# The feed-forward's two products in block form with seven block products for eight, in a two-layer decoder step on one core

## The chip, the cores and the metric

The kernel runs on one core of one Trainium2 chip. The metric is the device time of one execution in microseconds, as the median of several runs. Beside it one execution was taken with a profiler, and all stage times come from that one. Engines are named as in the profile: PE (TensorE matmuls), PEld (its weight loads), DVE (VectorE), ACT (ScalarE), POOL (GpSimd), SP (SyncE, which issues most transfers).

## The reference

One inference step of a decoder of two layers, on 1024 prompt tokens and 8 sample tokens (1032 columns together), with model width 1024 and feed-forward width 4096. Each layer has a token mixer (gated linear attention in layer 0, sliding-window attention in layer 1, each beside attention into a memory), an output projection, and a feed-forward part:

```python
def squared_relu_mlp(h, w_up, w_down):
    return jnp.square(jax.nn.relu(h @ w_up)) @ w_down
...
        x = x + rmsnorm(mix, norm_mix_post[l])
        f = squared_relu_mlp(rmsnorm(x, norm_ffn_pre[l]), w_ffn_up[l], w_ffn_down[l])
        x = x + rmsnorm(f, norm_ffn_post[l])
```

All inputs are float32. Between the layers one projection gives the keys and values for layer 1.

## The kernel before, in words

**Layout.** Activations lie with features on partitions: x is 8 tiles of 128 features, each with 1032 token columns. The columns are cut into three chunks of 384, 384 and 264 (`CH`). A weight tile is 128 x 8 x 128: for one tile of 128 output features (up) it holds all 8 tiles of input features, and for one tile of 128 inner features (down) all 8 tiles of outputs.

**Precision.** Every operand of a large product is split in two parts of type fp32r: a high part, which ACT casts (`wh`, `xh`), and a low part, which DVE makes as the source minus the high part (`wl`, `xl`; function `split`, lines 146 and 147). A product is three matmuls: high by high, high weight by low x, low weight by high x (`proj`, lines 227 to 229). So one up-tile on one chunk is 8 x 3 matmuls.

**The feed-forward (`mlp`).** The 32 tiles of the inner width are taken in eleven groups of two or three (`FF_GROUPS`). For a group, `up` makes the inner rows of one chunk: 24 matmuls per tile into a PSUM buffer, then DVE forms max(p, 0) times r (r is the reciprocal root-mean-square of the token, multiplied in here, line 520), ACT squares it twice, once in float32 and once as the high part, and POOL subtracts for the low part (lines 523 to 525). `down` takes a group's inner rows as moving operand, 3 matmuls per tile and output tile (lines 544 to 546), and DVE adds the result of each output tile to the sum F in SBUF (line 553; ACT copies for the first group, line 550). The order alternates up and down over chunks and groups, so that PE always has a product whose operands have been ready for long. The inner activations never leave SBUF. In layer 0, POOL also multiplies twelve weight tiles of layer 1 by the norm's gains during this stage (`fold`, line 220).

**The closing of a chunk (`Residual`).** ACT squares F, DVE adds up, PE sums over partitions with a matrix of ones (line 185), ACT and DVE make the reciprocal root (lines 188 to 192), DVE scales F, multiplies by the gain and adds the residual, which SP loads from DRAM (lines 294 to 301). In layer 1 the result goes to the output; in layer 0 it is split again as next operand, and `measure` makes the next r.

**What orders the work.** Instructions are written out once, and a planner orders them on each engine by the order in the program, where `high_priority` moves a block ahead by so many instructions (evictions of PSUM by 400, weight loads by `WPRI`, 1500), and it sets the waits. A buffer of a pool is handed on when every user of the tile in it is done. Engines run their own queues in order.

**Buffers.** PSUM has two buffers for products in `pm` and four more in the feed-forward. Weight staging (`wp`) has two raw tiles, `wA` three split ones.

Of the kernel before, what the change touches and what calls it, by code (L numbers as in the profile page):

```python
# [8 lines left out]
F32 = mybir.dt.float32  # L9
# [9 lines left out]
KT = 8  # L19
# [14 lines left out]
FF_GROUPS = [3, 2] + [3] * 9  # L34
# [7 lines left out]
def hybrid_decoder_step(ctx: ExitStack, tc: tile.TileContext, A, O):  # L42
# [37 lines left out]
    mvd = dram.tile([2, P, 2, MEM], F32, tag="mvd", name="mvd")  # L80

# [81 lines left out]
    class Stats:  # L163
        def __init__(self, n, tag="sf"):
            self.n = n
            self.tag = tag
            self.acc = None
            self.extra = []

        def add(self, x):  # L170
            t = view(tp.tile([P, 768], F32, tag="tq", name=nm("tq")), [P, 2, self.n])
            nc.scalar.activation(t, x, AF.Square)
            if self.acc is None:
                self.acc = t
            else:
                TT(self.acc, self.acc, t, ALU.add)  # L176
# [17 lines left out]
    def wload(pool, src, pri=WPRI):  # L194
        with tc.high_priority(pri):
# [4 lines left out]
            split(wh, wl, ws)  # L200
# [15 lines left out]
    def fold(i):  # L216
        src, g = (A["w_kv"][i], G_KV) if i < 4 else (A["w_in_b"][i - 4], G_MIXPRE + 1)
        ws = wp.tile([P, KT, P], F32, tag="ws", name=nm("wf"))
# [22 lines left out]
    class Residual:  # L241
# [22 lines left out]
        def finish(self, bf):  # L264
# [15 lines left out]
            def load(j):  # L280
# [4 lines left out]
                xs = xsp[0].tile([P, 2, 384], F32, tag="xs", name=nm("xs"))[:, :, :n]  # L285
                nc.sync.dma_start(xs, self.xsrc[:, 2 * j : 2 * j + 2, c0 : c0 + n])
                got.append(xs)

            for j in range(4 if self.last else 2):
                load(j)  # L290
            for j in range(4):
# [10 lines left out]
                if j < 2:  # L302
                    load(j + 2)
# [142 lines left out]
    def out_proj(l, make_o, src_pool, st, xsrc, psum=True):  # L446
        wO = st.enter_context(tc.tile_pool(name=nm("wO"), bufs=5, reuse_waits="tile"))
        f0 = st.enter_context(tc.tile_pool(name=nm("fo"), bufs=1, reuse_waits="tile"))
# [30 lines left out]
        f1 = st.enter_context(tc.tile_pool(name=nm("fo"), bufs=1, side="right", reuse_waits="tile"))  # L479
        f2 = st.enter_context(tc.tile_pool(name=nm("fo"), bufs=1, side="right", reuse_waits="tile"))  # L480
        xsp[0] = st.enter_context(tc.tile_pool(name=nm("xs"), bufs=2, side="right", reuse_waits="tile"))
# [8 lines left out]
        R[2].measure(5.5 * unit)  # L490
        set_extra(None, 0)
        return res

    def mlp(l, X):
        with ExitStack() as st:
            xsp[0] = st.enter_context(tc.tile_pool(name=nm("xs"), bufs=2, side="right", reuse_waits="tile"))
            fp = st.enter_context(tc.tile_pool(name=nm("ff"), bufs=1, side="right", reuse_waits="tile"))
            ap = st.enter_context(tc.tile_pool(name=nm("fa"), bufs=6, reuse_waits="tile"))
            wB = st.enter_context(tc.tile_pool(name=nm("fw"), bufs=4, reuse_waits="tile"))
            set_extra(st.enter_context(tc.tile_pool(name=nm("pmx"), bufs=4, space=PSUM, reuse_waits="tile")), 4)  # L500
            F = [fp.tile([P, KT, CH[c][1]], F32, tag=f"f{c}", name=nm("f")) for c in (2, 1, 0)][::-1]
            groups = []
            m0 = 0
            for g in FF_GROUPS:
                groups.append(list(range(m0, m0 + g)))
                m0 += g
            ups, dns, acts = {}, {}, {}

            def up(gi, c):
                if c == 0:  # L510
                    ups[gi] = [wload(wA, A["w_up"][l, m]) for m in groups[gi]]
                hl, r = X[c]
                n = CH[c][1]
                res = []
                for w in ups[gi]:
                    ps = mmps()
                    proj(ps, w, hl, n)
                    with first():
                        t = tmp3([P, 2, n])
                        STT(t[:, 0, :], ps[:, :n], 0.0, r, ALU.max, ALU.mult)  # L520
                        ah = ap.tile([P, n], F32R, tag="ah", name=nm("ah"))
                        al = ap.tile([P, n], F32R, tag="al", name=nm("al"))
                        nc.scalar.activation(t[:, 1, :], t[:, 0, :], AF.Square)  # L523
                        nc.scalar.activation(ah, t[:, 0, :], AF.Square)  # L524
                        nc.gpsimd.tensor_tensor(al, t[:, 1, :], f32(ah), ALU.subtract)  # L525
                    res.append((ah, al))
                acts[gi, c] = res

            R = {}

            def down(gi, c):
                if gi == L:
                    R[c] = Residual(c, F[c], G_FFNPOST + l, xd, last=(l == 1))
                if c == 0:
                    dns[gi] = [wload(wB, A["w_down"][l, m]) for m in groups[gi]]
                n = CH[c][1]
                a = acts.pop((gi, c))
                ng = len(a)
                for m in range(KT):
                    ps = mmps()  # L540
                    for k in range(ng):
                        wh, wl = dns[gi][k]
                        ah, al = a[k]
# [4 lines left out]
                    if gi == 0:  # L548
                        with first():
                            nc.scalar.copy(F[c][:, m, :], ps[:, :n])  # L550
# [932 lines left out]
```

## Time and profile before

| | |
|---|---|
| median of 3 runs | 2422.64 us (2418.98 to 2424.86) |
| the profiled execution | 2415.36 us |
| its span, first to last instruction | 2413.6 us |
| granted TensorE clock, mean | 0.99 |
| feed-forward of layer 0 | from 544.4 to 1271.2 us |
| feed-forward of layer 1 | from 1668.7 to 2395.8 us |

A row of the profile's groups has the line of the code, the engine, the operation, its output and inputs with their shapes, the count, then busy time, the mean of one in ns, and the idle time before it with what ended it. In a row by time the first number is the start, the second the duration in us. In a row by stretch come the stretch and its length, then the busy time and the count on PE, PEld, DVE, ACT and POOL, the granted clock, the DMA share and GB/s. A matmul's duration overlaps that of the next one; what it costs is the distance from start to start.

### The profile page before, as it was taken

The numbers are of one execution on the slowest core, as the hardware profiler recorded it, in microseconds if no ns is written. First come the engines' busy times: TensorE is split into PE (matmuls) and PEld (weight loads), VectorE is DVE, ScalarE is ACT, GpSimd is POOL, SyncE is SP. The second block draws the span as 40 slices with busy tenths as digits, with TensorE's granted clock in tenths as the row PEclk, the third lists the DMA queues.
The fourth block names the chain that finished last, engine by engine and source line by source line (L and its number), as shares of the span: only waits on it lengthen the run. The fifth ranks groups of instructions, "written<-read, shape, count | busy, mean of one in ns | idle before, by whom it ended". The sixth has DMA issues, their size and how long they took to land. (4 is left out here: it accounts for less than half of the span.)

```text
span 2413.6 us, 36268 instructions
## 1 busy us (share of the span) xinstructions
PE 2338.5 (97%) x14996; PEld 2221.0 (92%) x14996; DVE 1140.8 (47%) x2180; ACT 816.8 (34%) x1762; POOL 267.5 (11%) x270
## 2 busy tenths in 40 slices
PE   7999999899999999999998999899999999999997
PEld 6769998899999999999998878599999999999997
DVE  7544547666333333333368355647333333333337
ACT  6442535445222112221234355545422121221224
POOL 0001100002122112211110000200111111111121
PEclk9999999999999999999999999999999999999998
DMA  5321016433122122211125101324211111111123
GB/s 195 127 86 56 20 62 157 129 122 116 62 88 71 62 79 88 88 53 36 53 67 158 49 18 46 98 70 141 63 53 36 53 53 53 53 33 38 53 63 114
DMA packets 82799, 184.64 MB, mean 77 GB/s; under 512 B 7754, under 2 KB 49811, under 8 KB 82339
## 3 DMA queue, kind: packets, MB, share of 16 engines
q1 hardware_dynamic: 69522, 156.27, 20.9%
q0 software_dynamic: 3312, 13.30, 1.8%
q10 hardware_dynamic: 9792, 12.68, 1.4%
q8 instruction: 119, 1.95, 0.3%
q14 instruction: 54, 0.44, 0.1%
HBM read 150.79 MB, written 33.51 MB: 76 GB/s over the span
## 5 line engine op out<-in xcount | busy, mean ns | idle before, releaser
L227 PE MATMUL mm<-xh,wh 128*128 128x384 f32 (+3 forms) x1344 | 434.5, 324 | 18.2 <-ACT wh L146 12.0
L227 PE MATMUL mx<-xh,wh 128*128 128x384 f32 (+2 forms) x1344 | 430.4, 320 | 4.2 <-ACT wh L146 2.3
L228 PE MATMUL mx<-xl,wh 128*128 128x384 f32 (+2 forms) x1344 | 430.6, 321 | 3.5 <-DVE xl L598 2.0
L229 PE MATMUL mm<-xh,wl 128*128 128x384 f32 (+3 forms) x1344 | 432.1, 322 | 0.3 <-DVE wl L147 0.3
L228 PE MATMUL mm<-xl,wh 128*128 128x384 f32 (+3 forms) x1344 | 431.8, 321 | 0.0
L229 PE MATMUL mx<-xh,wl 128*128 128x384 f32 (+2 forms) x1344 | 430.2, 320 | 0.0
L146 ACT CAST wh<-ws 128x1024 fp32r<-128x1024 f32 x186 | 193.1, 1049 | 584.8 <-PE mx L228 204.6
L525 POOL TENSOR_TENSOR al<-t,ah 128x384 fp32r<-128x384 f32 (+1 forms) x192 | 204.5, 1065 | 1550.1 <-ACT ah L524 1349.8
L545 PE MATMUL mx<-al,wh 128*128 128x384 f32 (+1 forms) x1015 | 321.4, 317 | 0.3 <-POOL al L525 0.3
L544 PE MATMUL mx<-ah,wh 128*128 128x384 f32 (+1 forms) x1015 | 321.4, 317 | 0.0
L546 PE MATMUL mx<-ah,wl 128*128 128x384 f32 (+1 forms) x1015 | 321.1, 316 | 0.0
L147 DVE TENSOR_TENSOR wl<-ws,wh 128x1024 fp32r<-128x1024 f32 x186 | 226.8, 1229 | 115.1 <-ACT wh L146 115.0
L523 ACT ACTIVATE t<-t 128x384 f32<-128x384 f32 (+1 forms) x192 | 94.0, 490 | 544.5 <-DVE t L520 544.4
L227 PEld LDWEIGHTS mm<-xh,wh 128*128 128x128 f32 (+2 forms) x1344 | 249.6, 186 | 28.9 <-ACT wh L146 12.5
L228 PEld LDWEIGHTS mx<-xl,wh 128*128 128x128 f32 (+1 forms) x1344 | 253.3, 188 | 7.0 <-DVE xl L598 3.6
L227 PEld LDWEIGHTS mx<-xh,wh 128*128 128x128 f32 (+1 forms) x1344 | 253.1, 188 | 6.6 <-ACT wh L146 2.5
L553 DVE TENSOR_TENSOR f<-mx,f 128x384 f32<-128x384 f32 (+1 forms) x318 | 162.6, 514 | 202.5 <-PE mx L546 202.0
L229 PEld LDWEIGHTS mm<-xh,wl 128*128 128x128 f32 (+2 forms) x1344 | 249.4, 186 | 8.7 <-issue 6.5
L228 PEld LDWEIGHTS mm<-xl,wh 128*128 128x128 f32 (+2 forms) x1344 | 250.0, 186 | 7.5 <-issue 5.4
L229 PEld LDWEIGHTS mx<-xh,wl 128*128 128x128 f32 (+1 forms) x1344 | 253.1, 188 | 1.6 <-issue 1.0
L520 DVE SCALAR_TENSOR_TENSOR t<-mx,r 128x384 f32<-128x384 f32 (+1 forms) x131 | 67.5, 516 | 338.5 <-PE mx L229 320.7
L545 PEld LDWEIGHTS mx<-al,wh 128*128 128x128 f32 x1015 | 190.4, 188 | 0.7 <-POOL al L525 0.5
(370 smaller groups left out, 3301.5 us busy)
## 6 DMA issues: line engine op xcount, KB each, us to landing
ws<-in_w_up SPq DMA_DIRECT2D x64, 512.0 KB, 3.7
ws<-in_w_down SPq DMA_DIRECT2D x64, 512.0 KB, 3.7
ws<-in_w_in_a SPq DMA_DIRECT2D x22, 512.0 KB, 3.7
xd<-f ACTq DMA_DIRECT2D x24, 384.0 KB, 4.7
ws<-in_w_out SPq DMA_DIRECT2D x16, 512.0 KB, 3.7
xs<-xd SPq DMA_DIRECT2D x16, 384.0 KB, 4.2
wfd<-wf SPq DMA_DIRECT2D x12, 512.0 KB, 2.6
ws<-wfd SPq DMA_DIRECT2D x12, 512.0 KB, 3.9
```

The costliest lines, as they stand in the source:

```text
L146: nc.scalar.copy(hi, src)
L147: (eng or nc.vector).tensor_tensor(lo, src, f32(hi), ALU.subtract)
L227: nc.tensor.matmul(ps[:M, :n], wh[:, k, :M], xh[:, k, :], start=(k == 0), stop=False)
L228: nc.tensor.matmul(ps[:M, :n], wh[:, k, :M], xl[:, k, :], start=False, stop=False)
L229: mm = nc.tensor.matmul(ps[:M, :n], wl[:, k, :M], xh[:, k, :], start=False, stop=(k == KT - 1))
L520: STT(t[:, 0, :], ps[:, :n], 0.0, r, ALU.max, ALU.mult)
L523: nc.scalar.activation(t[:, 1, :], t[:, 0, :], AF.Square)
L525: nc.gpsimd.tensor_tensor(al, t[:, 1, :], f32(ah), ALU.subtract)
L544: nc.tensor.matmul(ps[:, :n], wh[:, m, :], ah, start=(k == 0), stop=False)
L545: nc.tensor.matmul(ps[:, :n], wh[:, m, :], al, start=False, stop=False)
L546: mm = nc.tensor.matmul(ps[:, :n], wl[:, m, :], ah, start=False, stop=(k == ng - 1))
L553: TT(F[c][:, m, :], ps[:, :n], F[c][:, m, :], ALU.add)
```

## The change

Both products of the feed-forward are computed in 2 x 2 blocks by the form of Winograd, with seven block products and fifteen block sums in the place of eight block products. This holds for 28 of the 32 tiles of the inner width, in 14 pairs (`PAIRS`); the first four tiles (`NPL`) are computed as before, at the beginning of the up-product and at the end of the down-product. The up-product of all pairs comes first, then the down-product; the squared inner rows go to DRAM (`awd`, and `apd` for the four plain tiles) and are read back.

**Up.** The weight of a pair is 2 x 2 blocks (two output tiles by two halves of the input features), x is 2 x 2 blocks (two halves of the features by two halves of the columns, 516 each; the columns are those of chunks 0 and 1, and the two halves of chunk 2). The combinations of x are made once per layer: x is first scaled by gain and r (`scale`, on ACT and POOL, for chunk 2 on DVE), then combined in place and split seven times (`steps`, in a wide piece of 384 columns and a narrow one of 132). The combinations of the weights are made for each pair on POOL (`wino_weights`), each followed by a split on ACT and DVE. A block product is 4 x 3 matmuls on each of two halves of 258 columns (`SUB`).

**Down.** The pairs are taken in groups of 3, 3, 3, 3 and 2 (`DGROUPS`). A phase is one of the seven block products of a group, over four output tiles and two halves: 8 PSUM buffers of 3 x 3 matmuls (or 2 x 3). For each phase and pair the weight block is combined (POOL) and split, the block of inner rows is combined (POOL) and split. Seven sums of 4 x 516 are kept in SBUF; DVE adds each PSUM buffer to them. In the last group the seven sums are combined into the four blocks of the output (`phase`, 28 additions on DVE). Then the four plain tiles run over the three chunks, and DVE adds the blocks on eviction.

```diff
+NPL = 4
+HALF = NT // 2
+SUB = HALF // 2
+PAIRS = [(m, m + 1) for m in range(NPL, DFF // P, 2)]
+DGROUPS = [list(range(j, min(j + 3, len(PAIRS)))) for j in range(0, len(PAIRS), 3)]
+ORDER = (1, 7, 6, 5, 2, 3, 4)
...
+    class Slots:
...
+        def next(self):
+            self.half ^= 1
+            if self.half == 0:
+                self.cur = (self.kept or self.makers)[self.i % len(self.makers)]
+                if not self.kept:
+                    self.cur = self.cur()
+                self.i += 1
+            ks = slice(4 * self.half, 4 * self.half + 4)
+            return self.cur[0][:, ks, :], self.cur[1][:, ks, :]
...
+    def wino_weights(a11, a12, a21, a22, slots):
+        PT = nc.gpsimd.tensor_tensor
+
+        def cut(x):
+            hi, lo = slots.next()
+            split(hi, lo, x)
+            return hi, lo
+
+        yield cut(a11)
+        PT(a11, a11, a21, ALU.subtract)
+        PT(a21, a21, a22, ALU.add)
+        yield cut(a11)
+        PT(a11, a22, a11, ALU.subtract)
+        yield cut(a11)
+        yield cut(a21)
+        w = cut(a12)
+        PT(a12, a12, a11, ALU.subtract)
+        yield w
+        yield cut(a12)
+        yield cut(a22)
...
+        def steps(p):
+            cut(1, "b11", p)
+            comb(p, "b12", "b22", "b12", ALU.subtract)
+            yield
+            cut(7, "b12", p)
+            comb(p, "b11", "b12", "b11", ALU.add)
+            yield
...
+        def triple(ps, wh, wl, hl_of, n):
+            for k in range(n):
+                xh, xl = hl_of(k)
+                nc.tensor.matmul(ps, wh(k), xh, start=(k == 0), stop=False)
+                nc.tensor.matmul(ps, wh(k), xl, start=False, stop=False)
+                mm = nc.tensor.matmul(ps, wl(k), xh, start=False, stop=(k == n - 1))
+            tick(mm, 3 * n * SUB)
...
+        def product(j, i, a, tmp):
...
+            for s in range(2):
+                ps = mmps()[:, :SUB]
+                triple(ps, lambda k: wh[:, k, :], lambda k: wl[:, k, :],
+                       lambda k: (sub(hi[:, k], s), sub(lo[k], s)), 4)
+                with first():
...
+                    elif i == 6:
+                        TT(sub(t("u4", "tq"), s), ps, sub(tmp["p1"], s), ALU.add)
+                        TT(sub(tmp["u3"], s), ps, sub(tmp["u3"], s), ALU.add)
...
+            with first():
+                for cc in {5: [c22], 2: [c11], 3: [c12], 4: [c21]}.get(i, []):
+                    STT(cc, cc, 0.0, cc, ALU.max, ALU.mult)
...
+            prepare(t + (3 if j == 0 else 7))
+            product(j, i, a, tmp)
+            if i == ORDER[-1]:
+                nc.sync.dma_start(awd[l, j], a)
...
+            def prep(self, i):
+                PT = nc.gpsimd.tensor_tensor
...
+                for q, gen in enumerate(self.gens):
+                    b11, b12, b21, b22 = self.blocks[q]
+                    w = next(gen)
+                    if i == 7:
+                        PT(b12, b22, b12, ALU.subtract)
+                    if i == 6:
+                        PT(b11, b12, b11, ALU.add)
+                    if i == 5:
+                        PT(b12, b22, b11, ALU.subtract)
+                    x = {1: b11, 7: b12, 6: b11, 5: b12, 2: b21, 3: b22, 4: b21}[i]
+                    h = homes[q]
+                    split(h[:, 0], h[:, 1], x)
+                    if i == 2:
+                        PT(b21, b11, b21, ALU.subtract)
+                    out.append((w, h))
+                return out
...
+            for mp in range(4):
+                for s in range(2):
+                    ps = mmps()[:, :SUB]
+                    triple(ps, lambda q: parts[q][0][0][:, mp, :], lambda q: parts[q][0][1][:, mp, :],
+                           lambda q: (sub(parts[q][1][:, 0], s), sub(parts[q][1][:, 1], s)), n)
+                    dst = sub(acc[i][:, mp], s)
                     with first():
...
+                        if gi == 0:
+                            nc.scalar.copy(dst, ps)
+                        else:
+                            TT(dst, ps, dst, ALU.add)
+            if gi != last:
+                return
+            for mp in range(4):
+                c = lambda k: acc[k][:, mp]
+                if i == 6:
+                    TT(c(6), c(6), c(1), ALU.add)
+                    TT(c(7), c(7), c(6), ALU.add)
...
+        for t in range(len(phases) - 1):
+            prep_phase(t + 1)
+            phase(t)
```

Smaller edits: the six weight tiles of the next projection (`wload` with `eng`) have their low parts made on POOL and not on DVE; the statistics of chunk 2 before the feed-forward are asked for 3.5 instead of 5.5 tile-products later; the residual is loaded to buffers that the feed-forward has freed; the output projection's result stays in SBUF, since the blocks of x are made from it.

476 lines of the change are left out of this document (376 added, 100 removed).

## The prediction

> **What bounds the kernel now.** I read the page from the top, then the stages around the feed-forward, then the distance from one matmul to the next, and last the groups by shape on the engines that get new work.
>
> ```profile
> span 2413.6 us, 36268 instructions
> PE 2338.5 (97%) x14996; PEld 2221.0 (92%) x14996; DVE 1140.8 (47%) x2180; ACT 816.8 (34%) x1762; POOL 267.5 (11%) x270
> ...
> PEclk9999999999999999999999999999999999999998
> ...
> 544.40:571.00 26.60, 24.78 (x132) 24.14 (x131) 21.04 (x34) 14.67 (x27) 3.77 (x3) 0.94 0.52 154
> 571.00:1200.00 629.00, 627.58 (x4023) 627.20 (x4022) 228.00 (x368) 143.41 (x260) 112.61 (x97) 1.00 0.21 70
> 1200.00:1271.30 71.30, 70.59 (x468) 69.68 (x467) 42.23 (x68) 22.88 (x35) 8.32 (x9) 1.00 0.22 71
> ```
>
> The last three rows are layer 0's feed-forward (stretch, its length, then busy PE, PEld, DVE, ACT, POOL, the granted clock, the DMA share, GB/s). PE is busy for 627.58 of 629.00 us at clock 1.00, and DVE for 228 of them. The stage, 544.40 to 1271.30, is 726.9 us of PE at work, and everything else hides under it. So fewer matmul columns shorten it, until another engine fails to keep up. "Busy" doesn't say what a matmul costs, since matmuls overlap; the distance between starts does:
>
> ```profile
> 799.79 0.33 PE L227 MATMUL mm<-xh,wh 128*128 128x384 f32 x1
> ...
> 801.70 0.34 PE L229 MATMUL mm<-xh,wl 128*128 128x384 f32 x1
> 801.87 0.28 PE L544 MATMUL mm<-ah,wh 128*128 128x264 f32 x1
> ...
> 805.96 0.28 PE L545 MATMUL mx<-al,wh 128*128 128x264 f32 x1
> ...
> 53.34 0.28 PE L227 MATMUL mx<-mh,wh 128*128 128x256 f32 x1
> ...
> 54.41 0.28 PE L227 MATMUL mx<-mh,wh 128*128 128x256 f32 x1
> ```
>
> Twelve matmuls of 384 columns lie from the first row to the second: 1.91 us over 11 steps, 0.1736 us each. From 801.87 to 805.96 are 34 steps of 264 columns, 0.1203 us. The 256-column stream in the last two rows makes 9 steps in 1.07 us, 0.119 us. The new products have 258 columns, between the last two: I take 0.119.
>
> **The change part by part.** PE first. Before, each layer has, for each of the two products, 32 tiles by 8 by 3 matmuls on each of three chunks: 3072 of 384 columns and 1536 of 264 columns in all, 533.3 + 184.8 = 718.1 us; the stage's 726.9 holds 8.8 us more (statistics, gaps), which I keep. After: four plain tiles in both products, 384 x 0.1736 + 192 x 0.1203 = 89.8 us; and 14 pairs by 7 products by 4 blocks by 2 halves by 3, twice, 4704 matmuls x 0.119 = 559.8 us. Together 649.6: PE has 68.5 us less per layer, 137 us in both. That is only 9.5% of the stage, not one eighth of 28/32, because the count of matmuls grows with 258 columns in the place of 384.
>
> A rule stands against this. The Trainium skill, page "TensorE: Matmul & The Clock Gate", section "Back-to-back issue gap", gives for sustained weight-load and matmul pairs about 81 ns at 128 columns and 131 ns at 512. Estimated from these by a straight line, 384, 264 and 258 columns would cost 114, 99 and 98 ns, the layer 502 us before and 524 after: slower. The rows above (174 and 120 ns) disagree.
>
> What goes on the other engines (relu products, squares and the 240 sums of a layer) was hidden under PE, so its going is worth nothing by itself. What they get instead is priced from these groups (busy, then mean ns of one):
>
> ```profile
> L147 DVE TENSOR_TENSOR wl<-ws,wh 128x1024 fp32r<-128x1024 f32 x186 | 226.8, 1229 | 115.1 <-ACT wh L146 115.0
> L147 DVE TENSOR_TENSOR xl<-f,xh 128x768 fp32r<-128x768 f32 x8 | 7.6, 949 | 0.8 <-ACT xh L146 0.8
> L553 DVE TENSOR_TENSOR f<-mx,f 128x264 f32<-128x264 f32 x108 | 46.3, 432 | 57.6 <-PE mx L546 57.5
> L146 ACT CAST wh<-ws 128x1024 fp32r<-128x1024 f32 x186 | 193.1, 1049 | 584.8 <-PE mx L228 204.6 <-PE mm L228 149.8 <-PE mx L545 78.3
> L525 POOL TENSOR_TENSOR al<-t,ah 128x384 fp32r<-128x384 f32 x128 | 134.5, 1051 | 1135.6 <-ACT ah L524 980.0 <-DVE xl L311 133.1 <-issue 22.5
> L946 POOL TENSOR_TENSOR qk<-qk,tq 96x512 f32<-96x512 f32 x8 | 10.3, 1283 | 13.4 <-ACT tq L931 13.4
> L220 POOL TENSOR_TENSOR wf<-wf,gains 128x1024 f32<-128x1024 f32 x12 | 22.8, 1898 | 59.6 <-DMA wf<-in_w_in_b 34.5 <-DVE t L520 23.0 <-DMA wf<-in_w_kv 1.5
> ...
> 2380.34 1.82 DVE L296 TENSOR_TENSOR f<-f,xall 128x768 f32<-128x768 f32 x2
> 2382.07 1.51 DVE L294 TENSOR_TENSOR f<-f,rf 128x768 f32<-128x768 f32 x1
> ...
> 2381.34 1.43 POOL L525 TENSOR_TENSOR al<-t,ah 128x264 fp32r<-128x264 f32 x1 [25.97 <-ACT ah L524]
> ...
> 1257.17 1.77 DVE L147 TENSOR_TENSOR wl<-ws,wh 128x1024 fp32r<-128x1024 f32 x1
> ...
> 1257.04 0.82 POOL L525 TENSOR_TENSOR al<-t,ah 128x264 fp32r<-128x264 f32 x1 [27.46 <-ACT ah L524]
> ```
>
> DVE from SBUF is 0.949 us for 768 and 1.229 for 1024 elements, so 0.67 for the new 512 and 516; in a row each is some 0.04 shorter (two of 768 take 1.82), I use 0.63. An eviction of 258 columns: 0.42 alone, 0.38 in a row. ACT: 0.6 for 512. POOL: 1.28 for 512, the L946 row.
>
> The last five rows hold the point that matters most. A DVE operation with two SBUF inputs that starts while POOL works is late by what POOL has left: the split at 1257.17 took 1.77 instead of 1.23 us (POOL ended at 1257.86), the product at 2382.07 took 1.51 instead of 0.91 (POOL until 2382.77). POOL suffers as well: 1.43 us behind two DVE operations, 0.82 where it came first. So POOL's combinations and DVE's splits take turns. The Trainium skill, "SBUF — State Buffer", section "Who interferes with whom", states this as a lock held for a whole instruction; the trace agrees with it on operations with two SBUF inputs. If it were no lock, the slower rival below would lose its mechanism.
>
> *Up-product.* Per pair: 16 evictions, 4 squares (516), 7 weight splits (512) on DVE, 16 x 0.38 + 11 x 0.63 = 13.0 us; POOL 4 x 1.28 and in layer 0 a fold of 1.9, 7.0 us; PE 168 x 0.119 = 20.0. Turns on the shared path 11 x 0.63 + 7.0 = 13.9. The splits are issued seven products ahead. All is hidden: 0 per layer, at most 10 if a pair waits 0.7 us.
>
> *Its start.* The blocks of x are scaled, combined and split while four plain tiles run (44.9 us) and in the first pair (20). DVE: five splits and four combinations of the wide piece, 10 x 0.95 + 4 x 1.82 = 16.8; the same of the narrow one and its scaling, about 11 by the 264-column row; the pair's own 13.0; and what already keeps DVE busy there, 21.04 of 26.60 us in the first stretch. Together some 62 of 65 us, with POOL in turns (8 scalings between 1.3 and 1.9 us, two splits). Between 0 and 20; I take 6, since PE is reached only by the last part of it. Chunk 2's statistics are asked for two tile-products sooner (3.5 for 5.5): chunk 0's plain tiles cover them, 0, at most 2 inside this bound.
>
> *Between the products.* The down-product's first blocks go to the homes of the last block of x, free two products (5.7 us) before the end; its weights' slot is that of the last product. The nearest transfers:
>
> ```profile
> ws<-in_w_up SPq DMA_DIRECT2D x64, 512.0 KB, 3.7
> ...
> xs<-xd SPq DMA_DIRECT2D x8, 264.0 KB, 3.7
> ```
>
> The loads (264 KB each, then 512 KB) take 3.7 us, more when nine queue up; then ACT 0.6, and nine POOL operations (11.5 us) before the second phase, whose forerunner lasts 8.6. Between 1 and 15, I take 5. The activations' way out and back adds 30 MB per layer, 45 GB/s on top of 70, under the 154 of the first stretch: hidden, or at most inside the 15.
>
> *Down-product, four groups of three pairs.* A phase is 72 matmuls, 8.57 us. DVE: six splits and eight evictions, 6 x 0.63 + 8 x 0.38 = 6.8 us. POOL: 24 combinations per group, 30.7 us, in bursts (9, 6, 3, 6 in four of seven phases). Taking turns: 42 x 0.63 + 30.7 = 57.2 of 60.0 us. The chain POOL, ACT, DVE runs one phase ahead of PE. It fits by 3 us on the mean, not in the bursts: the 9 take 11.5 us plus DVE's turns against about 12 us from the middle of the phase before. Also every second phase waits to split its third weight, whose slot is shared with a half of the phase just ending. Nothing if DVE goes between, up to 10 per group; I take 2.5, near the lower end because the mean fits: 10.
>
> *Last group, of two pairs.* A phase is 48 matmuls, 5.71 us; DVE needs 4 x 0.63 + 8 x 0.38 = 5.6, and the block sums come on top: 8, 8, 4 and 4 operations of 0.63 after phases three to six. The next phase's splits queue behind them on DVE, and PE waits for those: 4.9 + 4.9 + 2.4. Then the plain tiles' splits (4 x 1.23 + 2 x 0.95) and the sums against one phase: 6.7. Sum 18.9, with POOL's turns up to 28; at least 10 if sums are put off. I take 20.
>
> *Plain tiles, tail, hand-over.* Chunk 1's closing work has 11.5 us of matmuls (96 x 0.1203) as cover where it had 17.3; POOL instead of DVE splits the next layer's six weights (six turns of 1.9 us, hidden by 25 us of the first chunk's matmuls). 0 to 8; I take 3.
>
> Losses per layer: 0 + 6 + 5 + 10 + 20 + 3 = 44 against 68.5, bounds 11 and 121. Net 24.5, 49 us in both: the span goes to 2364.6 and its execution (2415.36, 1.8 above its span) to 2366.4. The median of the runs, 2422.64, lies 7.3 above that execution; on its scale the time is 2373.6, **2374 us**, 2.0% less.
>
> **The rivals.** *PE stays the bound.* If DVE and POOL slot in as smoothly as now (228 busy of 629), only the low bounds remain: 2422.6 - 2 x (68.5 - 11) = 2308, at best 2286. For it: PE's 99.8% now. Against it: the last group's sums alone exceed their cover. *DVE blocked by POOL becomes the down-product's bound: slower.* Let x be the share of POOL's 30.7 us per group in which DVE stands still. DVE then needs 42 x 0.63 + 56 x 0.38 = 47.7 and 30.7x against 60, the bound from x = 0.4; four groups lose 4 x (30.7x - 12.3), the last 18.9 + 20.5x. With 14 us for the rest the 68.5 are used up at x = 0.59; at 0.7 the loss is 84 per layer and the time 2454, at 0.8 it is 2483. For it: the two delayed rows. Against it: evictions can run beside POOL. *A matmul costs mostly its issue, not its columns.* Then 5280 matmuls in the place of 4608 outweigh: at the mean distance of now the layer's 718 us become 823, and the time 2633 before any loss. The three streams speak against it; only a weight load that is slower in these products could bring it. (By the figures of the Trainium skill's page "TensorE: Matmul & The Clock Gate" above, the two layers would take 44 us longer than before: some 2467.) *The count isn't reduced*: the loops fix it; time as before.
>
> **How the numbers follow.** Forecast 0.53, own range 2335 to 2425; PE-bound 0.20; blocked DVE 0.24; issue-bound 0.02; not as said 0.01. A measurement of this kernel can tell about 0.3% (7 us) from no change. Faster: 0.49 of the forecast and PE-bound, 0.69. Within 0.3%: the forecast's upper edge 0.04, the third case's lower edge 0.02, and the last 0.01, 0.07. Slower 0.24. The range leaves out half of the PE-bound case and a tenth at the top: 2300 to 2445.
>
> **What would show it.** Right: 258-column matmuls 0.119 us apart; up-stretches with PE gaps only in the first pair; in the down-product gaps ended by DVE's splits (or POOL), 2 to 3 us per full group, some 20 in the last. Wrong: gaps in every phase ended by DVE with splits near 1.2 us instead of 0.67 (blocked DVE), steps over 0.125 us (issue), or none at all in the last group (PE-bound). A transfer that lands late between the products would add what I have not priced.

## The result and the profile after

The kernel after takes 2476.24 us (median of 4 runs, 2474.82 to 2477.93), the kernel before on the same chip 2420.81 (2416.91 to 2424.86): ratio 1.0229, 95% interval 1.0209 to 1.0249. It is slower, where the forecast was 2374 us and faster. The profiled execution took 2475.34 us.

First the page after: the span, the engines, the granted clock in 40 slices.

```profile
span 2473.6 us, 41200 instructions
PE 2276.5 (92%) x16340; PEld 2138.5 (86%) x16340; DVE 1760.0 (71%) x3214; ACT 967.3 (39%) x2098; POOL 651.9 (26%) x460
...
PEclk9999999999999998999998999999899998999988
```

PE has fallen from 97% to 92% of a longer span: it works less, as intended, and stands more. POOL went from 267.5 to 651.9 us. Where PE stands is read from layer 0's stages (stretch, length, then busy PE, PEld, DVE, ACT, POOL, clock, DMA share, GB/s):

```profile
546.00:611.00 65.00, 50.71 (x297) 49.64 (x296) 59.37 (x78) 33.13 (x60) 26.98 (x13) 0.89 0.37 118
611.00:649.00 38.00, 26.87 (x174) 24.93 (x173) 36.20 (x52) 13.90 (x32) 20.66 (x15) 0.87 0.40 132
...
720.00:922.00 202.00, 201.98 (x1684) 201.74 (x1683) 135.36 (x273) 46.27 (x90) 55.42 (x41) 1.00 0.34 119
922.00:955.50 33.50, 22.79 (x148) 21.16 (x148) 16.38 (x18) 12.76 (x29) 21.72 (x15) 0.80 0.73 277
...
999.00:1197.00 198.00, 187.15 (x1513) 184.68 (x1512) 184.97 (x292) 68.22 (x126) 110.60 (x72) 0.98 0.28 86
1197.00:1250.50 53.50, 46.66 (x339) 45.18 (x338) 50.66 (x103) 16.67 (x28) 16.82 (x10) 0.90 0.06 21
1250.50:1303.30 52.80, 49.46 (x293) 47.99 (x292) 43.26 (x74) 17.28 (x22) 2.42 (x1) 0.94 0.44 136
```

These are the plain up-tiles, the first pair, ten pairs in the steady state, the passage between the products, groups 2 to 4 of the down-product, the last group, and the plain down-tiles. Of these stages only the steady up-product (201.98 of 202.00) keeps PE full. In groups 2 to 4 DVE is busy for 184.97 of 198 us and POOL for 110.60, where before DVE had 228 of 629.

Against what the matmuls alone need, by the starts of the block matmuls in the trace (0.120 us a step, 20.1 us a pair of the up-product, 60.3 a full group, 40.2 the last one, 44.9 the plain tiles of a product):

| us beyond the matmuls | forecast (bounds) | layer 0 | layer 1 |
|---|---|---|---|
| plain up-tiles, then up-product | 6 (0 to 30) | 20.1 + 28.7 | 17.2 + 12.5 |
| between the products (first two phases) | 5 (1 to 15) | 16.0 | 15.3 |
| the rest of the four full groups | 10 (0 to 40) | 17.8 | 17.8 |
| last group | 20 (10 to 28) | 13.1 | 14.4 |
| plain down-tiles, then hand-over or tail | 3 (0 to 8) | 7.8 + 12.7 | 9.6 + 2.0 |
| sum | 44 | 116.2 | 88.8 |

The last two columns also hold the 8.8 us per layer that the old stage had beyond its matmuls; so 116.2 + 88.8 - 2 x 8.8 = 187.4 us are lost. PE saves 718.1 - 654.2 = 63.9 us per layer at 0.120 us a step, 127.8 in both. The difference, 59.6, fits the 60.0 us by which the span grew (2473.6 - 2413.6), as well as rounded steps allow, which is to 2 or 3 us.

What PE waited for most in groups 2 to 4 of layer 0 (total, times, longest):

```profile
PE mx L709 <- DVE wl L154: 6.1, 4, 2.5
```

Of PE's 10.8 us of waits there, 10.3 end with one of DVE's splits. By the starts of the matmuls, the steps that hold a wait lose 12.9 us, and slower steps behind them 4.2 (see the last section).

DVE's instructions in the same stretch, by shape (count, then busy, mean ns):

```profile
L154 DVE TENSOR_TENSOR af<-ar,af 128x516 fp32r<-128x516 f32 x63 | 68.3, 1084 | 0.0
L901 DVE TENSOR_TENSOR acc<-mx,acc 128x258 f32<-128x258 f32 x111 | 44.5, 416 | 6.7 <-PE mx L709 6.6
L154 DVE TENSOR_TENSOR wl<-arw,wh 128x512 fp32r<-128x512 f32 x41 | 44.4, 1082 | 2.7 <-ACT wh L153 2.7
L154 DVE TENSOR_TENSOR wl<-ws,wh 128x512 fp32r<-128x512 f32 x21 | 25.0, 1192 | 0.2 <-ACT wh L153 0.2
```

The 125 splits take 137.7 us, 1.10 each, where the forecast had 0.67 alone and 0.63 in a row. Why, a stretch of group 2 shows, row by row (start, duration), DVE first, then POOL:

```profile
1030.59 1.74 DVE L154 TENSOR_TENSOR af<-ar,af 128x516 fp32r<-128x516 f32 x1
1032.26 0.41 DVE L901 TENSOR_TENSOR acc<-mx,acc 128x258 f32<-128x258 f32 x1
1032.59 1.67 DVE L154 TENSOR_TENSOR wl<-arw,wh 128x512 fp32r<-128x512 f32 x1
```

```profile
1030.48 1.30 POOL L569 TENSOR_TENSOR ws<-ws,ws 128x512 f32<-128x512 f32 x1 [13.48 <-DVE wl L154]
1032.41 1.30 POOL L859 TENSOR_TENSOR ar<-ar 128x516 f32<-128x516 f32 x1 [0.63 <-DVE af L154]
1034.40 1.29 POOL L569 TENSOR_TENSOR arw<-arw 128x512 f32<-128x512 f32 x1 [0.69 <-DVE wl L154]
```

Each of these splits starts 0.1 to 0.2 us after a POOL combination and ends about 0.55 us after that combination does: POOL's 1.30, then the split's own work. The eviction behind it, which reads one operand from PSUM and is not slowed itself (0.41), waits in DVE's queue until the split is done. A split on DVE releases the next combination, which is in place, and the next split runs into that again.

### The profile page after: what moved, and what is told of

Same layout as the page of the kernel before. It is cut to its first block, busy times and chain, and to the rows that moved or that the text cites. A ratio compares the mean times of both kernels' runs of the same rounds, so it can differ in the third digit from the quotient of the medians.

```text
span 2473.6 us, 41200 instructions
## 1 busy us (share of the span) xinstructions
PE 2276.5 (92%) x16340; PEld 2138.5 (86%) x16340; DVE 1760.0 (71%) x3214; ACT 967.3 (39%) x2098; POOL 651.9 (26%) x460
## 5 line engine op out<-in xcount | busy, mean ns | idle before, releaser
L153 ACT CAST wh<-ws 128x512 fp32r<-128x512 f32 (+1 forms) x286 | 202.3, 721 | 586.4 <-POOL ws L569 109.7
L154 DVE TENSOR_TENSOR wl<-ws,wh 128x512 fp32r<-128x512 f32 (+1 forms) x280 | 267.3, 956 | 176.2 <-ACT wh L153 173.9
L708 PE MATMUL mx<-af,wh 128*128 128x258 f32 x1034 | 300.6, 291 | 14.2 <-DVE af L154 14.2
L235 PE MATMUL mm<-xh,wh 128*128 128x384 f32 (+3 forms) x904 | 296.3, 328 | 15.8 <-ACT wh L153 12.7
L709 PE MATMUL mx<-af,wl 128*128 128x258 f32 x1034 | 299.5, 290 | 9.9 <-DVE wl L154 9.9
L707 PE MATMUL mx<-af,wh 128*128 128x258 f32 x1034 | 296.5, 289 | 9.0 <-ACT af L153 7.1
L708 PE MATMUL mx<-xf,wh 128*128 128x258 f32 x792 | 227.8, 288 | 9.4 <-DVE xf L154 9.4
L707 PE MATMUL mx<-xf,wh 128*128 128x258 f32 x792 | 228.1, 288 | 5.7 <-DVE u L746 4.3
L709 PE MATMUL mx<-xf,wl 128*128 128x258 f32 x792 | 227.2, 287 | 5.4 <-DVE wl L154 5.4
L708 PEld LDWEIGHTS mx<-af,wh 128*128 128x128 f32 x1034 | 203.2, 197 | 17.0 <-DVE af L154 17.0
L709 PEld LDWEIGHTS mx<-af,wl 128*128 128x128 f32 x1034 | 203.3, 197 | 11.9 <-DVE wl L154 11.9
L707 PEld LDWEIGHTS mx<-af,wh 128*128 128x128 f32 x1034 | 200.0, 195 | 10.4 <-ACT af L153 7.3
L154 DVE TENSOR_TENSOR af<-ar,af 128x516 fp32r<-128x516 f32 x194 | 203.6, 1055 | 1.2 <-ACT af L153 0.8
L235 PEld LDWEIGHTS mm<-xh,wh 128*128 128x128 f32 (+1 forms) x904 | 167.7, 186 | 26.0 <-ACT wh L153 12.7
L708 PEld LDWEIGHTS mx<-xf,wh 128*128 128x128 f32 x792 | 153.4, 194 | 10.5 <-DVE xf L154 10.5
L707 PEld LDWEIGHTS mx<-xf,wh 128*128 128x128 f32 x792 | 152.9, 193 | 6.6 <-DVE u L746 4.7
```

What stands on the lines that cost most here:

```text
L153: nc.scalar.copy(hi, src)
L154: (eng or nc.vector).tensor_tensor(lo, src, f32(hi), ALU.subtract)
L235: nc.tensor.matmul(ps[:M, :n], wh[:, k, :M], xh[:, k, :], start=(k == 0), stop=False)
L707: nc.tensor.matmul(ps, wh(k), xh, start=(k == 0), stop=False)
L708: nc.tensor.matmul(ps, wh(k), xl, start=False, stop=False)
L709: mm = nc.tensor.matmul(ps, wl(k), xh, start=False, stop=(k == n - 1))
```

## The experiments

The theory, **turns** (A in the expectations): DVE's splits and POOL's combinations take turns on a shared path, and DVE's queue stands meanwhile. The rivals: **POOL's results** (C), for which the splits wait, and not for its turn; **transfers and buffers**, which hold PE up; and **DVE's own work** (B), too much for it. Each run is one execution unless said otherwise. The kernel before took 2420.29 us beside e1 to e4, and 2411.95 beside e5 to e8, so whole times from the two sets compare only to within some 8 us; the stages are surer.

**e1_no_comb.** All combinations on POOL are left out (weights and inner rows); splits, transfers and matmuls stay.

```diff
-        PT = nc.gpsimd.tensor_tensor
+        PT = lambda *x: None
...
-                PT = nc.gpsimd.tensor_tensor
+                PT = lambda *x: None
```

> All combinations of weight blocks and inner-row blocks on POOL are left out in the block products (the blocks are split and multiplied uncombined). Theory A, POOL's operations hold up DVE's splits: the down-product's splits fall from about 1.1 us to 0.67 to 0.70, groups two to four of the down-product take 181 us together (198 in the changed kernel), the first two phases lose under 4 us in the place of 16, the last group still loses 10 or more by its sums; the whole about 2400 us. Theory B, DVE has too much work of its own: the splits fall too, but groups two to four stay over 190 us. Theory C, PE waits for POOL's results and not for DVE's lock: 181 us as in A, but e2 must then show the same.

Measured: 2394.5 us. Groups 2 to 4 of layer 0, DVE by shape and then the stretch:

```profile
L901 DVE TENSOR_TENSOR acc<-mx,acc 128x258 f32<-128x258 f32 x115 | 48.6, 424 | 23.3 <-PE mx L709 22.9
L154 DVE TENSOR_TENSOR af<-ar,af 128x516 fp32r<-128x516 f32 x61 | 42.0, 688 | 0.0
L154 DVE TENSOR_TENSOR wl<-arw,wh 128x512 fp32r<-128x512 f32 x42 | 28.7, 684 | 4.7 <-ACT wh L153 4.7
...
L154 DVE TENSOR_TENSOR wl<-ws,wh 128x512 fp32r<-128x512 f32 x22 | 15.0, 683 | 0.5 <-ACT wh L153 0.5
```

```profile
980.00:1160.00 180.00, 180.00 (x1506) 180.00 (x1505) 139.98 (x296) 68.53 (x128) 0.00 (x0) 1.00 0.29 95
```

The same 125 splits take 85.7 us, 0.69 each: 52.0 us less, 17.3 per group. PE is busy for 180.00 of 180.00; groups 2 to 4 last 60.3 us each. So neither transfers and buffers nor DVE's own work (139.98 of 180) bound the full groups of the kernel after. The evictions didn't change (0.424 against 0.416). The two phases between the products lose 8.2 and 4.9 us instead of 16.0 and 15.3, so about half of that loss or more is POOL's. The up-product, whose weight blocks go uncombined as well, takes about 294 and 289 us instead of 311 and 295, though the folds are still on POOL. The plain up-tiles did not change (66.2 and 62.1; after 65.0 and 62.1), nor did the last group much (52.0 and 50.7; after 53.3 and 54.6): these losses have other causes than the combinations.

**e2_comb_idle.** The down-product's combinations run on POOL as in the kernel after, but write to a spare tile that nothing reads; the blocks go uncombined into the product.

```diff
-        PT = nc.gpsimd.tensor_tensor
+        PT = lambda o, a, b, op: nc.gpsimd.tensor_tensor(o2(o) if o2 else o, a, b, op)
```

> In the down-product POOL makes every combination from the same sources but writes it to a spare tile that nobody reads; the blocks are multiplied uncombined. Theory A: POOL still takes turns with DVE, splits stay over 1.0 us and groups two to four take 190 us or more. Theory C: nobody waits for POOL's results any more, so groups two to four fall to about 181 us although the splits stay long. Up-product as in the changed kernel.

Measured: 2481.1 us.

```profile
L154 DVE TENSOR_TENSOR af<-ar,af 128x516 fp32r<-128x516 f32 x62 | 66.4, 1072 | 0.0
```

```profile
1000.00:1200.00 200.00, 186.64 (x1495) 184.16 (x1495) 180.09 (x292) 64.86 (x121) 107.37 (x70) 0.97 0.27 85
```

Nobody waits for POOL's results, and still the splits take 1.07 us and groups 2 to 4 last 66.6 to 69.9 us (after 64.6 to 67.8). So it is POOL's activity beside DVE, not the wait for its data: the turns hold, and the wait for POOL's results falls as cause in the full groups. (Why they are even a little longer than in the kernel after isn't shown. Buffers are still handed on only when POOL has read them, as in the kernel after.) Between the products it is otherwise: the first two phases lose 12.5 and 12.1 us here, 16.0 and 15.3 in the kernel after, 8.2 and 4.9 in e1. Of POOL's share, 3.5 and 3.2 us are thus the wait for its results, and 4.3 and 7.2 its activity.

**e3_comb_dve.** The combinations are made on DVE.

```diff
-        PT = nc.gpsimd.tensor_tensor
+        PT = nc.vector.tensor_tensor
...
-                PT = nc.gpsimd.tensor_tensor
+                PT = nc.vector.tensor_tensor
```

> The same combinations made on DVE in the place of POOL. Theory A: nobody shares the path, each costs DVE 0.63 us, a full group needs 62.8 us of DVE against 60 of PE, so groups two to four take 188 to 192 us (198 now), the first two phases lose 8 in the place of 16, the last group loses 5 to 10 more; the whole 2440 to 2465 us. Theory B: DVE is fuller still, groups two to four 205 us or more, the whole over 2480.

Measured: 2418.75 us, better than any theory had it.

```profile
L154 DVE TENSOR_TENSOR af<-ar,af 128x516 fp32r<-128x516 f32 x60 | 41.1, 687 | 0.1
...
L859 DVE TENSOR_TENSOR ar<-ar,ar 128x516 f32<-128x516 f32 x6 | 4.1, 687 | 0.0
```

```profile
985.00:1165.00 180.00, 180.00 (x1497) 179.38 (x1496) 174.93 (x356) 67.86 (x123) 0.00 (x0) 1.00 0.30 95
```

DVE has 336 instructions more over the run and is busy for 174.93 of 180 us, and PE is full again: the groups last 60.4 to 60.9. A combination on POOL costs DVE 0.72 us of standing (17.3 us for 24), and 0.69 to do it itself (the second row). Handing this work to POOL relieved DVE of nothing.

**e4_fold_act.** Only the multiplication of layer 1's weights by the gains (12 tiles, during layer 0) goes from POOL to ACT.

```diff
-        nc.gpsimd.tensor_tensor(ws, ws, gains[:, g, :].unsqueeze(2).to_broadcast([P, KT, P]), ALU.mult)
+        for k in range(KT):
+            nc.scalar.mul(ws[:, k, :], ws[:, k, :], gains[:, g, k : k + 1])
```

> The twelve weight tiles of the next projections are multiplied by their gains on ACT (eight operations of 128 columns each) in the place of POOL. Theory A: layer 0's up-product loses the 16 us or more that it takes longer than layer 1's (310.9 against 294.7 us for the block products), the whole 2455 to 2462 us. Theories B and C: DVE's own work or the block chain sets the start, the up-product stays over 305 us and the whole within 5 us of 2476.

Measured: 2462.7 us, 12.6 less than the profiled execution of after. Layer 0's up-product shrank from 310.9 to 298.0 us; the other stages stayed within 2.5 us. What the folds meet is seen in the kernel after, in POOL's groups from 546 to 649:

```profile
L228 POOL TENSOR_TENSOR wf<-wf,gains 128x1024 f32<-128x1024 f32 x5 | 15.4, 3079 | 7.7 <-DVE xl L331 6.5 <-DMA wf<-in_w_kv 1.2
L619 POOL TENSOR_TENSOR f<-f,r 128x768 f32<-128x768 f32 x6 | 12.4, 2088 | 26.8 <-ACT t L609 26.8
```

Five folds, 3.08 us each where they took 1.9 before, stand in the same turns as the blocks of x. Without the combinations and with the folds (e1) the up-product was shortened by as much, so POOL's load as a whole counts there, not the folds alone.

**e5_no_sums.** The 28 sums of a layer that combine the seven block sums are left out.

```diff
-            if gi != last:
-                return
+            return
```

> The changed kernel without the 28 additions that combine the seven sums in the last group (the output blocks stay uncombined). If the sums before the next phase's splits on DVE cause the last group's loss, as the prediction has it, the group takes 41 to 43 us instead of 53 to 55, the plain tiles behind it lose 2 to 4 us less, and the whole is 25 to 32 us faster (2445 to 2451). If POOL's turns cause it, the group stays at 48 us or more.

Measured: 2445.8 us. The last group lasts 42.9 us in both layers (after 53.3 and 54.6), the plain down-tiles 46.1 and 48.4 (52.7 and 54.5). So the sums cost 17.0 and 17.8 us per layer, three fifths of it in the last group and the rest after it. The whole is 29.6 us shorter and not 34.8, as layer 0's up-product and the hand-over came out 2.8 and 2.6 us longer.

**e6_start.** e3 with the fold on ACT as in e4, and the scaling of chunks 0 and 1 and all low parts of x on DVE. POOL is all but idle in the feed-forward (2.87 us from 545 to 1250).

```diff
-            if c < 2:
+            if False:
...
-            eng = nc.gpsimd if i in (2, 3) else nc.vector
+            eng = nc.vector
```

> As e3 (combinations on DVE), and POOL is taken out of the start: the fold on ACT, the scaling of x and all splits of its blocks on DVE. If POOL's turns make the start late, the plain tiles fall from 65.7 to about 55 us and the first pair from 38 to under 30 us, in layer 0 more than in layer 1; the whole 2385 to 2398 us against 2419 of e3. If DVE's own work bounds the start (it gets some 25 us more of it per layer), the gain is under 8 us, or the start is longer.

Measured: 2387.4 us. The plain up-tiles fell from 65.7 and 61.9 (e3) to 48.6 and 47.7. The up-product fell from about 302 to 297 us in layer 0 and rose from 294 to 297 in layer 1. In layer 1 of e3 the scaling and the low parts of x were all that POOL had in these tiles (there is no fold there), so taking them off POOL brought the 14.2 us; ACT's part of the scaling went to DVE with them, and this run doesn't tell the two apart. What is left of the start, 15 us, is nearly all in the first pair (34.6 and 35.1 for 20.1), which had been expected under 30.

**e7_last3.** e3 with the groups of the down-product as 2, 3, 3, 3, 3, so that the sums come beside a group of three pairs.

```diff
-DGROUPS = [list(range(j, min(j + 3, len(PAIRS)))) for j in range(0, len(PAIRS), 3)]
+DGROUPS = [list(range(max(j, 0), j + 3)) for j in range(-1, len(PAIRS), 3)]
```

> As e3, with the group of two pairs first and four groups of three behind it. If the last group's loss comes from DVE work per phase against PE time per phase, a phase of 8.6 us covers more of the sums: the last group loses 6 to 10 us (60.3 being none) where it lost 17 to 18, and the first phases wait for fewer transfers (the first group loses 4 to 6 in the place of 7); the whole 2395 to 2405 us. If the sums' own order costs it, the loss stays at 15 or more.

Measured: 2404.1 us. The last group now loses 15.4 and 14.4 us (75.7 and 74.7 for 60.3) instead of 18.1 and 17.1, the plain down-tiles last 47.8 and 49.2 instead of 52.7 and 53.1, and the first group loses 6.2 and 4.0 instead of 7.6 and 6.7. The longer phases thus gave the last group 2.7 us, where 7 or more had been expected: its loss stays near the 15 that was expected if the order of the sums itself costs it.

**e8_all.** e6 and e7 together, and the low parts of the next projection's six weights on DVE.

```diff
-                W = [wload(wA if i < 3 else wK, wfd[j], eng=nc.gpsimd) for i, j in enumerate((2, 3, 0, 1, 10, 11))]
+                W = [wload(wA if i < 3 else wK, wfd[j]) for i, j in enumerate((2, 3, 0, 1, 10, 11))]
```

> e6 and e7 together, and the low parts of the next layer's six weights on DVE as before the change. If the gains add, 2365 to 2385 us; if the start is bound by DVE, 2395 or more.

Measured: 2366.8 us. **e9_all_timed** is the same kernel once more, for an interval.

> The kernel of e8_all once more, unchanged, timed in five rounds against the kernel before, since one look (2366.78 us, before 2411.95 on that chip) has no interval. Theory (the block form itself saves PE 68.5 us per layer, and the loss came from POOL's turns on the shared path and from the crowded start and end): 2360 to 2375 us, ratio 0.978 to 0.984 of before. Rival (a good part of e8_all's gain was the luck of one look or of one chip): ratio above 0.99.

Measured: 2368.74 us (5 runs, 2363.09 to 2370.11) against 2417.63 for before (9 runs): ratio 0.9789, 95% interval 0.9773 to 0.9804. This version beats both kernels: the block form does pay, 2.1%, once POOL is out of it and the groups are ordered as in e7 (e6, without that order, took 2387.4 beside 2411.95). Its page, and three stretches (plain up-tiles, first pair, last group):

```profile
span 2368.3 us, 40946 instructions
...
PE 2243.3 (95%) x16340; PEld 2117.2 (89%) x16340; DVE 1783.4 (75%) x3612; ACT 991.7 (42%) x2162; POOL 40.6 (2%) x66
```

```profile
542.00:591.00 49.00, 47.33 (x298) 46.40 (x297) 48.60 (x92) 33.10 (x69) 0.00 (x0) 1.00 0.46 144
591.00:625.00 34.00, 23.96 (x166) 22.53 (x166) 32.85 (x63) 20.91 (x52) 0.00 (x0) 0.90 0.39 144
...
1117.00:1193.60 76.60, 67.97 (x510) 66.78 (x509) 71.95 (x141) 24.15 (x40) 0.00 (x0) 0.91 0.05 16
```

DVE is busy for 48.60 of 49.00, 32.85 of 34.00 and 71.95 of 76.60 us: in the start and in the last group DVE's own work is now the likely limit, read from these shares and not tested.

**e10_stat_later.** e9 with the three sums of statistics at the hand-over asked for later.

```diff
-                R[0].measure(1.0 * unit)
+                R[0].measure(4.0 * unit)
...
-            R[1].measure(3.0 * unit)
-            R[2].measure(4.0 * unit)
+            R[1].measure(6.0 * unit)
+            R[2].measure(7.0 * unit)
```

> e9_all_timed with one more change: at the end of layer 0's feed-forward the matmuls that sum up the statistics of chunks 0, 1 and 2 are put behind 4, 6 and 7 tile-products of later matmuls instead of 1, 3 and 4. In e8_all PE stood 11.3 us in front of the first of them (from 1257.1), waiting for a vector of VectorE that was ready at 1268.8, while the first part of chunk 1 had been split by 1262.5 to 1265. If PE was only held up by the order of its queue: the gap shrinks by 4 to 7 us and the time by as much, 2360 to 2364 on the scale of e8_all. If VectorE's chain for chunk 1 is what is late: the gap moves to the next matmul and the time stays within 2 us.

Measured: 2378.73 us (4 runs), ratio to before 0.9836, interval 0.982 to 0.9853: slower than e9 by 10 us, which neither branch of the expectation has. From the end of layer 0's feed-forward to the end of layer 1's output projection it takes 421.3 us against 411.3 in e9, 410.1 in after and 397.4 before. PE stood for 11.9 us in front of the statistics in e9; now it stands in front of the next product instead, for a weight that ACT casts late:

```profile
PE sA L236 <- ACT wh L153: 18.7, 1, 18.7
```

So asking for the sums later doesn't close the gap at the hand-over. POOL's six splits didn't matter there, as far as can be told: e8 and e9, one kernel without them, take 407.8 and 411.3. What the 13 us are made of stays open; DVE's chain for closing chunk 1, behind 11.5 us of matmuls instead of 17.3, is the likeliest and was not tried by itself.

## Why the prediction was wrong

**Right.** PE bounds the steady up-product, and 258 columns cost 0.120 us (0.119 forecast): the saving is 63.9 us per layer for 68.5. DVE's own need of 47.7 us in a full group was right too (139.98 / 3 = 46.7 in e1). The rival in which a matmul costs mostly its issue fell. The up-product from the sixth pair on runs at 20.1 us a pair, losing nothing, as priced. The sums of the last group, forecast at 18.9, cost 17.0 and 17.8 (e5), though they bite one phase later than said: phases of 5.8, 5.8, 6.0, 5.7, 11.9, 11.9 and 6.3 us for 5.7. The last group at 13 to 14 and the plain tiles after it at 8 to 10 share them.

**The step that failed** is the price of DVE's work beside POOL, written out for the four full groups: "Taking turns: 42 x 0.63 + 30.7 = 57.2 of 60.0 us", and from it "It fits by 3 us on the mean, not in the bursts". It treated the shared path as one resource and DVE's queue as another. But a split that has been started and blocked holds DVE's queue, with the evictions behind it: while POOL has its turn, DVE does nothing. The price of a split was thereby 1.10 us instead of 0.63 to 0.67. This is the rival "DVE blocked by POOL becomes the down-product's bound", with the forecast's own "Wrong" sign: gaps ended by DVE, and long splits. It had the mechanism, and its share x can now be read: 17.3 us of standing per group out of 30.7 us of combinations is x = 0.56. By its formula a group needs 47.7 + 17.3 = 65.0 us; 66.0 were measured (198 / 3). That it fits so well is partly luck: DVE was busy for 61.7 us of a group (184.97 / 3) and not throughout, and ten of the 21 phases are longer than 8.7 us, not each. Its row of evidence (a split of 1.77 us for 1.23, beside one POOL instruction) was in the profile before; the forecast took 2.5 us a group, "near the lower end because the mean fits", and 17.8 us a layer were lost there for its 10.

By size the forecast failed most at the start. The span exceeds the forecast's 2364.6 by 109.0 us. Against the forecast's terms, layers 0 and 1 together lose 66 us more in the start (17.6 us of gaps that the old stage had are counted here too), 21 between the products, 16 in the rest of the full groups and 26 in the plain down-tiles with hand-over and tail; the last group loses 12 less, and PE saves 9 less.

At x = 0.56 that rival alone, with its 14 us for the rest, would nearly have broken even. What made the kernel slower is above all that POOL's work was underpriced at two other places, by turns at the first and only in part by turns at the second:

- **The start**, taken at 6 us because "PE is reached only by the last part of it": 48.8 and 29.7. By the runs three things cost time in layer 0: POOL's scaling and low parts of x (14.2 us in layer 1, e6 against e3); the folds and the combinations, of which either alone, taken off POOL, shortens the up-product by 13 to 17 us (e4, e1), so that they don't simply add; and the first pair's own work on DVE, which remains at about 15 when POOL is idle (e6). DVE was busy or blocked for 59.37 + 36.20 of 103 us, where the sum had 62 of 65 without POOL's turns: so full an engine had no room for them. A scaling took 2.09 us, above the 1.3 to 1.9 given. The turns are seen here too. PE's first gap ends at 553.5 with a weight that ACT casts; ACT had waited for DVE, and DVE's operations had stood beside two scalings (the wait, then ACT's, DVE's and POOL's rows):

```profile
PE mm L235 <- ACT wx L153: 7.1, 1, 7.1
...
551.28 0.61 ACT L330 ACTIVATE xh<-f,gains 128x384 fp32r<-128x384 f32 x1 [5.14 <-DVE f L321]
...
544.65 2.20 DVE L331 SCALAR_TENSOR_TENSOR xl<-f,gains,xh 128x384 fp32r<-128x384 f32 x1
546.77 3.42 DVE L314 TENSOR_TENSOR f<-f,rf 128x768 f32<-128x768 f32 x2
...
544.27 4.23 POOL L619 TENSOR_TENSOR f<-f,r 128x768 f32<-128x768 f32 x2
```

  The operation that takes 2.20 us takes 0.61 at 550.11, where POOL is idle; a DVE split of 768 columns takes 1.25 us on the mean in the start, and 0.95 in e6.
- **Between the products**, taken at 5 us of 1 to 15: 16.0 and 15.3, at the upper bound. PE waits for ACT, and ACT for POOL. POOL makes six combinations of inner rows before a weight block of the third phase (L565), and ACT's cast of that block stands in its queue ahead of the casts of the second phase's inner rows. First the waits from 922 to 956 (total, times, longest), then POOL's rows and ACT's:

```profile
PE mx L707 <- ACT af L153: 7.1, 1, 7.1
ACT wh L153 <- POOL we L565: 5.5, 1, 5.5
```

```profile
928.52 1.29 POOL L850 TENSOR_TENSOR ar<-ar 128x516 f32<-128x516 f32 x1
...
938.33 1.26 POOL L565 TENSOR_TENSOR we<-we 128x512 f32<-128x512 f32 x1
...
939.62 0.62 ACT L153 CAST wh<-we 128x512 fp32r<-128x512 f32 x1 [5.48 <-POOL we L565]
940.14 3.23 ACT L153 CAST af<-ar 128x516 fp32r<-128x516 f32 x6
```

Of the six blocks cast from 940.14 on (the second and third phase's), the first had been ready since 929.81. The forecast had written down 11.5 us of POOL work before the second phase, but not that ACT's queue would make this phase wait for the third one's weight as well. In e2, where no cast waits for POOL's results, the six follow at 933.90. Without the combinations (e1) 8.2 and 4.9 us remain, near the 5 taken; in e1 ACT waits for 5.4 us for the inner rows' way through DRAM.

That every second phase waits for its third weight's slot costs nothing by itself: without the combinations every later phase of the full groups lasts 8.6 us (e1).

**Wrongly sized, and in part open**: the plain down-tiles with hand-over or tail, 20.5 and 11.6 us in a term of 3. Of the plain tiles' 7.8 and 9.6 us the sums are 6.6 and 6.1 (e5); what makes up the hand-over's 12.7 stays open.

With POOL idle (e6) the losses are, by the same table, 66 and 54 us per layer with the old gaps, 51 without them: close to the 44 forecast, but by luck in part. The start loses 18.7 and 17.9 us there for 6, the four full groups after their first two phases 1.2 for 10. As a sum, the forecast was that of a kernel without turns.

The Trainium skill, "SBUF — State Buffer", section "Who interferes with whom", has both halves of this: DVE with two SBUF inputs contends with a POOL instruction that reads SBUF, and DVE with one SBUF input does not. The runs agree: splits 1.10 us beside POOL and 0.69 without, evictions 0.416 and 0.424.

## What to carry to other kernels

When work moves to an engine that shares a path with a busy one, price it twice: once on the new engine, and once as standing time of the old one, whose whole queue stops behind the blocked instruction. A mean that fits by 5% says nothing if the two run in bursts, so ask what it costs to leave the work where it was; here 0.69 us on DVE was no dearer than 0.72 us of waiting for POOL to do it. And a change that only takes load from the bounding engine is worth what its start, its end and its seams leave over: here four fifths of some 100 us of losses per layer sat in a few stretches of 30 to 70 us, which a busy share over the whole stage does not show. Look there also for work of a later phase that stands in an engine's queue before what is needed now, as in ACT's between the products.

## What the runs showed of the hardware

A gap of PE cost more than its length here. In layer 1's plain up-tiles (1713.3 to 1775.4, 62.1 us for 44.9) there are two gaps; the waits, then PE's rows behind the first:

```profile
PE sx L193 <- DVE r L189: 5.5, 1, 5.5
PE sf L193 <- DVE rf L189: 5.1, 1, 5.1
```

```profile
1728.33 1.25 PE L193 MATMUL sf<-rf,ones 128*128 128x264 f32 x2 [5.13 <-DVE rf L189]
...
1730.01 0.53 PE L235 MATMUL mx<-xh,wh 128*128 128x384 f32 x1
1730.33 0.53 PE L236 MATMUL mx<-xl,wh 128*128 128x384 f32 x1
...
1734.97 0.34 PE L236 MATMUL mx<-xl,wx 128*128 128x384 f32 x1
1735.15 0.34 PE L237 MATMUL mx<-xh,wx 128*128 128x384 f32 x1
```

Behind the gap matmuls of 384 columns lie 0.32 us apart, later 0.18. The stretches give the granted clock (third figure from the end: 0.50 and 0.63):

```profile
1726.00:1732.00 6.00, 3.67 (x11) 3.47 (x12) 4.34 (x8) 4.37 (x9) 0.00 (x0) 0.50 0.24 92
...
1762.00:1768.00 6.00, 6.00 (x33) 5.86 (x32) 5.34 (x5) 3.77 (x7) 4.95 (x4) 0.63 0.09 33
```

The waits explain 10.6 of the 17.2 us lost there. The slow steps add about 2 us behind the first gap (from 1728.3 to about 1732 at half speed) and 6 x 0.37 = 2.2 behind the second; the rest, some 2.4 us, was not taken apart. The forecast priced waits by their length alone. The Trainium skill, "TensorE: Matmul & The Clock Gate", section "What's actually happening", says that the clock halves after an idle window of about 3.4 us and returns after about as long a busy one. The rows agree on the halving behind gaps of 5.1 and 5.5 us, and the slow steps last to 3.9 and 5.0 us after them. But a shorter wait in this trace was followed by slow steps too: PE stood for 2.52 us before 1143.96, and from 1145 to 1149 the clock was 0.57. So no idle window of 3.4 us was needed there.

POOL's instructions lengthen beside DVE as well: the fold of 1024 elements from 1.9 us before to 3.08 in the start, a combination of 512 from 1.28 to 1.54 on the mean of groups 2 to 4 (110.60 / 72).
